# Decoder trunk on one core: both query chunks accumulated in the input loop, ten zero products ahead, latent projection after it

## The chip, the cores and the metric

The kernel runs on one core of one Trainium2 chip. The metric is the device time of one launch in microseconds (us), the median over the runs. Each core has TensorE (PE, with its weight loads shown apart as PEld), VectorE (DVE), ScalarE (ACT), GpSimd (POOL) and SyncE (SP), and 16 DMA engines that all queues share.

## The reference, cut to what matters

The reference is one inference step of a two-layer decoder trunk for 512 prompt positions and 32 sample positions (8 sequences of 4). The first layer begins with one input projection of all 544 tokens; its first columns are the query latent (256) and the key/value latent with its rotary key (128 + 32):

```python
cq, ckv, kr, hf, hi, hq, hg = jnp.split(x @ w_in, [i1, i2, i3, i4, i5, i6], axis=-1)
q = (rms_norm(cq, g_q) @ w_uq).reshape(Bn, L, MLA_HEADS, NOPE_DIM + ROPE_DIM)
ckv = rms_norm(ckv, g_kv)
kr = apply_rope(kr, cos, sin)
```

The rest of the layer (latent attention, a gated linear recurrence, output projection, layer norm, a gated ConvFFN), the second layer and the outputs follow. All of it is float32; the input width is 1024, so a projection sums over 8 chunks of 128 input channels.

## The kernel before, in words

Every float32 operand of a projection is split in two parts that TensorE takes as float32r: a rounded part `hi` (ACT copies it, L144) and the rest `lo` (DVE subtracts, L138). One step of a projection is then three products, hi*hi, hi*lo and lo*hi, which `mm3` issues (L244 to L247). Tokens are held with channels on partitions, in two halves of 256 and 288 columns (`HALF`); the last 32 columns are the sample tokens.

The change lies in the first stage of layer one (L718 to L878). SP loads the tokens as they stand in memory (`xin`: four row blocks of 128 tokens, `xins`: the 32 sample tokens) with `load_x(c0, c1)` (L736), five DMAs for one range of columns, and weights with `load_w` (L741), one DMA each into a raw tile. There are four raw tiles (`WRAW`, tag `wraw`), so a fifth weight load waits until an earlier raw tile has been split; there are seven split pairs (`WHL`). `x_in(c)` (L772) takes input chunk c: per half, TensorE transposes two blocks of 128 tokens against the identity (and the sample tokens in the second half) into PSUM, and ACT and DVE split the result into `xh`, `xl`. That is five transposes and two splits for each chunk.

The loop at L786 goes over the 8 chunks. In chunk c it calls `x_in(c + 1)`, splits the weight tiles that begin with chunk c, and then issues 18 products: 6 for the first 128 query columns (`pcq`, 256 or 288 columns wide, the weight stationary) and 12 for the latent of the four prompt token blocks (`pck[t]`, 160 columns wide, the tokens stationary). Behind the loop stand the vectors' transposes (`pv`), the latent of the sample block (`pckv4`, 24 products, L812), the evacuation of the latents on ACT (`kv_done`), the evacuation of the first query chunk (`cq_done(0)`), and the second 128 query columns as a projection of its own (L830, 48 products with two weight loads of its own). Then `filler()` issues pieces of the next projection (`phi`), which fills TensorE while the norms are worked out: `pss` (20 products with a moving operand of one column, L841) sums the squared queries, POOL takes the inverse roots for queries and latents together, DVE scales the latents (L847) and TensorE transposes them (`plat`, L864).

What sets the order: the program is written in the order above, and the framework decides each engine's order when it builds the program, by the program's order and by what it takes to be ready by then. On the chip each engine then works its own list in that order. A split of a later weight can therefore stand on ACT ahead of a split of an earlier token chunk, and waits there for its load. POOL issues the loads of the small vectors (L755 to L762) and of the page table (L833, eight DMAs that broadcast one column of the table each) on a DMA queue of its own, without waiting for the stage.

Of the kernel before, what the change touches and what calls it, by code (L numbers as in the profile page):

```python
# [10 lines left out]
F32 = mybir.dt.float32  # L11
F32R = mybir.dt.float32r
# [12 lines left out]
KC = D // 128  # L25
# [16 lines left out]
HALF = ((0, 256), (256, 288))  # L42
# [3 lines left out]
GPACE = (1,)  # L46
NORMS = (((0, (3,)), (1, (3,))), ((2, (2, 3)), (3, (2, 3)), (4, (2, 3))))
WRAW = 4
WHL = 7

C_COS = 0
# [60 lines left out]
def trunk_kernel(ctx: ExitStack, tc: tile.TileContext, a, o):  # L112
    nc = tc.nc
    PS = bass.MemoryType.PSUM
    PE, ACT, DVE, POOL = nc.tensor, nc.scalar, nc.vector, nc.gpsimd
# [31 lines left out]
    def mmtile(name):  # L147
        pools = psum["mm"]
        pool = pools[turn_[0] // 2 % len(pools)]
        turn_[0] += 1  # L150
        return pool.tile([128, 512], F32, tag="mm", name=name)

    def axtile(name):
        return psum["ax"].tile([128, 512], F32, tag="ax", name=name)
# [55 lines left out]
    def wsplit(raw, w):  # L210
        hi = wp.tile([128, 512], F32R, tag="whi", name="whi", bufs=WHL)
        lo = wp.tile([128, 512], F32R, tag="wlo", name="wlo", bufs=WHL)
        split(raw[:, :w], hi[:, :w], lo[:, :w])
        return hi, lo
# [15 lines left out]
    def wkeys(wn, c0, kch, ncol=128):  # L230
        per = 512 // ncol
        return [(wn, c0, k, min(per, kch - k), ncol) for k in range(0, kch, per)]
# [9 lines left out]
    xh, xl = [], []  # L242

    def mm3(out, lh, ll, rh, rl, first, last):  # L244
        PE.matmul(out, lh, rh, start=first, stop=False)  # L245
        PE.matmul(out, lh, rl, start=False, stop=False)  # L246
        PE.matmul(out, ll, rh, start=False, stop=last)  # L247
# [24 lines left out]
    def proj(wn, c0, hs, ls, name, halves_apart=False):  # L272
        res = {}
        for _ in proj_steps(wn, c0, hs, ls, name, res, halves_apart):
            pass
        return res["ps"]
# [4 lines left out]
    def xtok(t_, t):  # L281
        hv, s0 = ((0, 0), (0, 128), (1, 0), (1, 128), (1, 160))[t]
        return t_[hv][:, s0:s0 + 128]
# [434 lines left out]
    with tc.tile_pool(name="p1", bufs=1) as p1:  # L718
# [7 lines left out]
        with tc.tile_pool(name="pa", bufs=1) as pa:  # L726
            xin = pa.tile([128, 4, D], F32, name="xin")
            xins = pa.tile([NS, D], F32, name="xins")
            v1 = pa.tile([128, 128], F32, name="v1")
            v2 = pa.tile([128, 128], F32, name="v2")  # L730
            v3 = pa.tile([128, 128], F32, name="v3")
# [4 lines left out]
            def load_x(c0, c1):  # L736
                for i in range(4):
                    nc.sync.dma_start(xin[:, i, c0:c1], a["x_prompt"][0, i * 128:(i + 1) * 128, c0:c1])
                nc.sync.dma_start(xins[:, c0:c1], xsv[:, c0:c1])

            def load_w(key):  # L741
                w0[key] = wload(*key)

            kq = wkeys(w_in, 0, KC)
            kkv = wkeys(w_in, QR, KC, 160)
            load_x(0, 256)
            load_w(kq[0])
            load_w(kkv[0])
            load_x(256, 512)
            load_x(512, 1024)  # L750
            load_w(kkv[1])
            load_w(kq[1])
            off = 0
            for nm, ap, n in vrows:
                nc.gpsimd.dma_start(v1[off:off + n, :], ap)  # L755
# [5 lines left out]
            nc.gpsimd.dma_start(v2, fcr[nfc:nfc + 128])  # L761
            nc.gpsimd.dma_start(v3[0:n3, :], fcr[nfc + 128:264])  # L762
            V["fc"] = off
            load_w(kkv[2])

            ckv = pa.tile([128, 5, 160], F32, name="ckv")
            ss = pa.tile([128, 10], F32, name="ss")
            junk = pa.tile([128, 128], F32, name="junk")
            pcq = [mmtile(f"cq0_{h}") for h in range(2)]
            pck = [axtile(f"pckv{t}") for t in range(4)]  # L770
            wq_, wkv = [], []
            def x_in(c):  # L772
                xh.append([])
# [10 lines left out]
                    xl[c].append(l_)  # L784
            x_in(0)
            for c in range(KC):  # L786
                if c + 1 < KC:
                    x_in(c + 1)
                for keys, ws in ((kq, wq_), (kkv, wkv)):
                    for key in keys:  # L790
                        if key[2] == c:
                            hi, lo = wsplit(w0[key], key[3] * key[4])
                            ws += [(hi[:, i * key[4]:(i + 1) * key[4]], lo[:, i * key[4]:(i + 1) * key[4]])
                                   for i in range(key[3])]
                for hv, (s0, n) in enumerate(HALF):
                    mm3(pcq[hv][:, :n], wq_[c][0], wq_[c][1], xh[c][hv], xl[c][hv], c == 0, c == KC - 1)
                for t in range(4):
                    mm3(pck[t][:, :160], xtok(xh[c], t), xtok(xl[c], t), wkv[c][0], wkv[c][1], c == 0, c == KC - 1)

            nc.sync.dma_start(gkv, a["g_kvnorm"][0].partition_broadcast(128))  # L800
            nc.sync.dma_start(cst, a["cst"])
# [6 lines left out]
            def kv_done(t, p):  # L808
                ACT.copy(ckv[:, t, :], p[:, :160])
                ACT.activation(junk, ckv[:, t, 0:128], AF.Square, scale=KVR ** -0.5, accum_out=ss[:, 5 + t:6 + t])  # L810

            p = axtile("pckv4")  # L812
            for k in range(KC):
                mm3(p[:, :160], xtok(xh[k], 4), xtok(xl[k], 4), wkv[k][0], wkv[k][1], k == 0, k == KC - 1)
            kv_done(4, p)
            for t in range(4):
                kv_done(t, pck[t])
            sqs = []

            def cq_done(c, ps):  # L820
# [5 lines left out]
                split(qg, qh[c], ql[c])  # L826
                sqs.append(sq)

            cq_done(0, [pcq[hv][:, :n] for hv, (s0, n) in enumerate(HALF)])
            cq_done(1, proj(w_in, 128, xh, xl, "cq"))  # L830
            pss = axtile("pss")
            for i in range(NPAGE):
                nc.gpsimd.dma_start(ptab[16 * i:16 * (i + 1), :], a["page_table"][:, i].partition_broadcast(16))  # L833
# [763 lines left out]
```

## Time and profile before

| | us |
|---|---|
| median of 3 runs | 1415.46 |
| lowest and highest run | 1415.35, 1423.20 |
| the profiled execution's own time | 1406.60 |
| its span, first to last instruction | 1404.90 |
| around the span | 1.70 |

The profiled execution was 8.86 us shorter than the median of the timed runs. In a timeline row the first number is the start in us from the span's start, the second is how long the instruction or the merged instructions took; after them come the engine, the line, the operation, out<-in, the shape and the count; the brackets give the idle time before it and what ended that. In a windows row each engine has its busy time in the stretch and its count of instructions; the last three columns are TensorE's granted clock (1.00 is full), the mean busy share of the 16 DMA engines, and what they moved. Products on TensorE overlap, so the pace is read from the starts of successive products and not from what one took. The granted clock is put together from recorded changes of it; ahead of the first recorded change the column shows 1.00.

### The profile page before, as it was taken

What the parts mean: (1) busy time and instruction counts of PE and PEld (TensorE: products, weight loads), DVE (VectorE), ACT (ScalarE), POOL (GpSimd) and SP (SyncE); (2) the same over time, 40 slices, a digit from 0 to 9 for tenths busy, and PEclk for the clock granted to TensorE, in tenths of its full rate; (3) what the DMA queues carried; (4) which work ended last, traced back from release to release, by engine and by line L of the source; (5) the groups of instructions that cost most, each with busy time, mean ns of one, the idle gap of its engine ahead of it and who ended that gap; (6) DMA issues with size and microseconds to landing.
All of it is one profiled execution on the core that took longest, in us unless ns stands there. A gap on an engine that the chain in (4) does not pass through costs nothing.

```text
span 1404.9 us, 28697 instructions
## 1 busy us (share of the span) xinstructions
PE 1358.8 (97%) x11130; PEld 1303.9 (93%) x11130; DVE 852.3 (61%) x1672; ACT 584.0 (42%) x1439; POOL 422.8 (30%) x623
## 2 busy tenths in 40 slices
PE   6999999987999999999999999999999999999995
PEld 5999996846999999999999989999999999999995
DVE  2348766566678667667332684457786676673335
ACT  2346663445455444443322453235444444432222
POOL 4003345364725222224411110067252122240004
PEclk9999999999999999999999999999999999999997
DMA  5213123312513332232233323224133332333321
GB/s 167 58 50 84 46 66 119 116 34 76 152 30 89 90 93 85 84 97 76 80 117 90 93 79 86 86 82 128 29 102 88 92 86 73 113 106 89 88 62 64
DMA packets 218245, 120.99 MB, mean 86 GB/s; under 512 B 11488, under 2 KB 213340, under 8 KB 218108
## 3 DMA queue, kind: packets, MB, share of 16 engines
q1 hardware_dynamic: 209068, 109.89, 27.3%
q0 software_dynamic: 2144, 5.43, 1.2%
q10 hardware_dynamic: 6896, 3.82, 0.9%
q8 instruction: 88, 1.44, 0.4%
q14 instruction: 49, 0.40, 0.1%
HBM read 113.25 MB, written 5.85 MB: 85 GB/s over the span
## 4 chain that ended last, share of the span: by engine, by line
PE 90%; DVE 3%; POOL 2%; ACT 2%; DMA 2%; issue 1%; SPq 0%; ACTq 0%; DVEq 0%; POOLq 0%
PE up L245 11%; PE up L246 11%; PE up L247 11%; PE f L245 6%; PE f L246 6%; PE f L247 6%; PE m L245 2%; PE m L247 2%; PE m L246 2%; PE up L438 1%; PE up L439 1%; PE up L436 1%; POOL xs L138 1%; PE sc L1151 1%; DMA wraw<-in_w_in_ab_dram 1%
## 5 line engine op out<-in xcount | busy, mean ns | idle before, releaser
L138 DVE TENSOR_TENSOR wlo<-wraw,whi 128x512 fp32r<-128x512 f32 (+1 forms) x371 | 268.0, 726 | 369.6 <-ACT whi L144 365.8
L144 ACT CAST whi<-wraw 128x512 fp32r<-128x512 f32 (+1 forms) x371 | 224.6, 609 | 474.4 <-issue 148.2
L245 PE MATMUL f<-gh,whi 128*128 128x256 f32 (+1 forms) x704 | 204.2, 290 | 0.0
L246 PE MATMUL f<-gl,whi 128*128 128x256 f32 (+1 forms) x704 | 203.1, 289 | 0.0
L247 PE MATMUL f<-gh,wlo 128*128 128x256 f32 (+1 forms) x704 | 201.9, 287 | 0.0
L245 PE MATMUL up<-m0h,whi 128*128 128x256 f32 (+1 forms) x640 | 185.0, 289 | 0.0
L246 PE MATMUL up<-m0l,whi 128*128 128x256 f32 (+1 forms) x640 | 184.6, 289 | 0.0
L247 PE MATMUL up<-m0h,wlo 128*128 128x256 f32 (+1 forms) x640 | 184.5, 289 | 0.0
L247 PE MATMUL up<-m1h,wlo 128*128 128x256 f32 (+1 forms) x640 | 184.5, 289 | 0.0
L245 PE MATMUL up<-m1h,whi 128*128 128x256 f32 (+1 forms) x640 | 184.4, 288 | 0.0
L246 PE MATMUL up<-m1l,whi 128*128 128x256 f32 (+1 forms) x640 | 184.4, 288 | 0.0
L247 PEld LDWEIGHTS f<-gh,wlo 128*128 128x128 f32 x704 | 132.6, 188 | 0.1
L246 PEld LDWEIGHTS f<-gl,whi 128*128 128x128 f32 x704 | 132.3, 188 | 0.1
L245 PEld LDWEIGHTS f<-gh,whi 128*128 128x128 f32 x704 | 132.1, 188 | 0.1
L245 PEld LDWEIGHTS up<-m0h,whi 128*128 128x128 f32 x640 | 120.5, 188 | 0.4 <-ACT hp L621 0.3
L245 PEld LDWEIGHTS up<-m1h,whi 128*128 128x128 f32 x640 | 120.5, 188 | 0.3 <-ACT hp L621 0.2
L246 PEld LDWEIGHTS up<-m0l,whi 128*128 128x128 f32 x640 | 120.7, 189 | 0.0
L246 PEld LDWEIGHTS up<-m1l,whi 128*128 128x128 f32 x640 | 120.4, 188 | 0.0
L247 PEld LDWEIGHTS up<-m1h,wlo 128*128 128x128 f32 x640 | 120.4, 188 | 0.0
L247 PEld LDWEIGHTS up<-m0h,wlo 128*128 128x128 f32 x640 | 120.3, 188 | 0.0
L629 POOL COPY stp<-hp 128x2 f32<-128x2 f32 x88 | 40.4, 460 | 208.1 <-ACT hp L622 208.1
L620 POOL COPY hp<-pf 128x18 f32<-128x18 f32 x88 | 49.0, 563 | 130.4 <-DVE co L559 119.6
(676 smaller groups left out, 3374.4 us busy)
## 6 DMA issues: line engine op xcount, KB each, us to landing
wraw<-in_ffn_w_up_dram SPq DMA_DIRECT2D x176, 256.0 KB, 2.9
wraw<-in_ffn_w_down_dram SPq DMA_DIRECT2D x80, 256.0 KB, 2.7
wraw<-in_w_in_cd_dram SPq DMA_DIRECT2D x40, 256.0 KB, 2.8
wraw<-in_w_in_ab_dram SPq DMA_DIRECT2D x36, 256.0 KB, 2.9
wraw<-in_w_out_ab_dram SPq DMA_DIRECT2D x16, 256.0 KB, 3.0
wraw<-in_w_out_cd_dram SPq DMA_DIRECT2D x16, 256.0 KB, 3.0
sti<-in_state_hgrn_dram SPq DMA_DIRECT2D x4, 512.0 KB, 4.0
out_hg_s_dram<-sti ACTq DMA_DIRECT2D x4, 512.0 KB, 3.3
```

The source lines that it names most:

```text
L138: eng.tensor_tensor(out, in0, in1, op)
L144: ACT.copy(hi, src)
L245: PE.matmul(out, lh, rh, start=first, stop=False)
L246: PE.matmul(out, lh, rl, start=False, stop=False)
L247: PE.matmul(out, ll, rh, start=False, stop=last)
L436: PE.matmul(out, hi[:, s], xh_, start=(k == 0 and not (shared and i % 2)), stop=False, skip_group_check=shared)
L438: PE.matmul(out, hi[:, s], xl_, start=False, stop=False, skip_group_check=shared)
L439: PE.matmul(out, lo[:, s], xh_, start=False, stop=(k == KC - 1), skip_group_check=shared)
L620: POOL.tensor_copy(pre, pf[:, c, :].rearrange("p (b r) -> p b r", r=2))
L629: POOL.tensor_copy(stp[:, :, c], hp[:, HPW - 2:HPW])
L1151: PE.matmul(sc[q_][32 * bb:32 * bb + 32, :], qlt[:, 4 * g + bb, :], ltT_, start=False, stop=True)
```

## The change

The loads of the tokens are cut at columns 128, 384 and 640 (four times five DMAs where there were three times five), and a weight tile holds two input chunks of all 256 query columns (four tiles) where it held four chunks of 128 columns. The loads are issued tokens and query weights in turn, the latent weights after them. A tile of zeros is set by DVE, and ten products of 512 columns of it, into a PSUM tile that nothing reads, stand ahead of the loop. In the loop each chunk has 12 products of 256 or 288 columns, for both query chunks. The latents of all five token blocks, 24 products each, come after the loop and after the evacuation of the queries.

```diff
@@ -46,6 +46,7 @@
 GPACE = (1,)
 NORMS = (((0, (3,)), (1, (3,))), ((2, (2, 3)), (3, (2, 3)), (4, (2, 3))))
 WRAW = 4
+NWARM = 10
 WHL = 7
 
 C_COS = 0
@@ -726,6 +727,8 @@
         with tc.tile_pool(name="pa", bufs=1) as pa:
             xin = pa.tile([128, 4, D], F32, name="xin")
             xins = pa.tile([NS, D], F32, name="xins")
+            warm = pa.tile([128, 512], F32R, name="warm")
+            DVE.memset(warm.bitcast(F32), 0.0)
             v1 = pa.tile([128, 128], F32, name="v1")
             v2 = pa.tile([128, 128], F32, name="v2")
             v3 = pa.tile([128, 128], F32, name="v3")
@@ -741,15 +744,18 @@
             def load_w(key):
                 w0[key] = wload(*key)
 
-            kq = wkeys(w_in, 0, KC)
+            kq = wkeys(w_in, 0, KC, 256)
             kkv = wkeys(w_in, QR, KC, 160)
-            load_x(0, 256)
+            load_x(0, 128)
             load_w(kq[0])
-            load_w(kkv[0])
-            load_x(256, 512)
-            load_x(512, 1024)
-            load_w(kkv[1])
+            load_x(128, 384)
             load_w(kq[1])
+            load_x(384, 640)
+            load_w(kq[2])
+            load_x(640, 1024)
+            load_w(kq[3])
+            for key in kkv:
+                load_w(key)
             off = 0
             for nm, ap, n in vrows:
                 nc.gpsimd.dma_start(v1[off:off + n, :], ap)
@@ -761,13 +767,14 @@
             nc.gpsimd.dma_start(v2, fcr[nfc:nfc + 128])
             nc.gpsimd.dma_start(v3[0:n3, :], fcr[nfc + 128:264])
             V["fc"] = off
-            load_w(kkv[2])
 
             ckv = pa.tile([128, 5, 160], F32, name="ckv")
             ss = pa.tile([128, 10], F32, name="ss")
             junk = pa.tile([128, 128], F32, name="junk")
-            pcq = [mmtile(f"cq0_{h}") for h in range(2)]
-            pck = [axtile(f"pckv{t}") for t in range(4)]
+            idle = axtile("idle")
+            for i in range(NWARM):
+                PE.matmul(idle, warm[:, 0:128], warm, start=True, stop=True)
+            pcq = [[mmtile(f"cq0_{h}") for h in range(2)], [axtile(f"cq1_{h}") for h in range(2)]]
             wq_, wkv = [], []
             def x_in(c):
                 xh.append([])
@@ -784,18 +791,16 @@
                     xl[c].append(l_)
             x_in(0)
             for c in range(KC):
+                if c % 2 == 0:
+                    hi, lo = wsplit(w0[kq[c // 2]], 512)
+                    wq_ += [(hi[:, i * 256:(i + 1) * 256], lo[:, i * 256:(i + 1) * 256]) for i in range(2)]
                 if c + 1 < KC:
                     x_in(c + 1)
-                for keys, ws in ((kq, wq_), (kkv, wkv)):
-                    for key in keys:
-                        if key[2] == c:
-                            hi, lo = wsplit(w0[key], key[3] * key[4])
-                            ws += [(hi[:, i * key[4]:(i + 1) * key[4]], lo[:, i * key[4]:(i + 1) * key[4]])
-                                   for i in range(key[3])]
-                for hv, (s0, n) in enumerate(HALF):
-                    mm3(pcq[hv][:, :n], wq_[c][0], wq_[c][1], xh[c][hv], xl[c][hv], c == 0, c == KC - 1)
-                for t in range(4):
-                    mm3(pck[t][:, :160], xtok(xh[c], t), xtok(xl[c], t), wkv[c][0], wkv[c][1], c == 0, c == KC - 1)
+                for j in range(2):
+                    js = slice(j * 128, (j + 1) * 128)
+                    for hv, (s0, n) in enumerate(HALF):
+                        mm3(pcq[j][hv][:, :n], wq_[c][0][:, js], wq_[c][1][:, js], xh[c][hv], xl[c][hv],
+                            c == 0, c == KC - 1)
 
             nc.sync.dma_start(gkv, a["g_kvnorm"][0].partition_broadcast(128))
             nc.sync.dma_start(cst, a["cst"])
@@ -809,12 +814,6 @@
                 ACT.copy(ckv[:, t, :], p[:, :160])
                 ACT.activation(junk, ckv[:, t, 0:128], AF.Square, scale=KVR ** -0.5, accum_out=ss[:, 5 + t:6 + t])
 
-            p = axtile("pckv4")
-            for k in range(KC):
-                mm3(p[:, :160], xtok(xh[k], 4), xtok(xl[k], 4), wkv[k][0], wkv[k][1], k == 0, k == KC - 1)
-            kv_done(4, p)
-            for t in range(4):
-                kv_done(t, pck[t])
             sqs = []
 
             def cq_done(c, ps):
@@ -826,8 +825,16 @@
                 split(qg, qh[c], ql[c])
                 sqs.append(sq)
 
-            cq_done(0, [pcq[hv][:, :n] for hv, (s0, n) in enumerate(HALF)])
-            cq_done(1, proj(w_in, 128, xh, xl, "cq"))
+            for key in kkv:
+                hi, lo = wsplit(w0[key], key[3] * 160)
+                wkv += [(hi[:, i * 160:(i + 1) * 160], lo[:, i * 160:(i + 1) * 160]) for i in range(key[3])]
+            for j in range(2):
+                cq_done(j, [pcq[j][hv][:, :n] for hv, (s0, n) in enumerate(HALF)])
+            for t in range(5):
+                p = axtile(f"pckv{t}")
+                for k in range(KC):
+                    mm3(p[:, :160], xtok(xh[k], t), xtok(xl[k], t), wkv[k][0], wkv[k][1], k == 0, k == KC - 1)
+                kv_done(t, p)
             pss = axtile("pss")
             for i in range(NPAGE):
                 nc.gpsimd.dma_start(ptab[16 * i:16 * (i + 1), :], a["page_table"][:, i].partition_broadcast(16))
```

## Rows read from the trace of the kernel before

**Rows 1.** The page: TensorE's busy line, and the chain that ended last by engine.

```profile
PE 1358.8 (97%) x11130; PEld 1303.9 (93%) x11130; DVE 852.3 (61%) x1672; ACT 584.0 (42%) x1439; POOL 422.8 (30%) x623
...
PE 90%; DVE 3%; POOL 2%; ACT 2%; DMA 2%; issue 1%; SPq 0%; ACTq 0%; DVEq 0%; POOLq 0%
```

**Rows 2.** Windows by stage: start:end, length, busy time of each engine, clock, DMA.

```profile
core 0: us, PE busy (x) PEld busy (x) DVE busy (x) ACT busy (x) POOL busy (x), PEclk, DMA share, GB/s
0.00:8.50 8.50, 3.29 (x11) 1.81 (x11) 0.98 (x2) 2.83 (x5) 7.79 (x23) 1.00 0.70 197
8.50:18.30 9.80, 9.62 (x41) 8.89 (x41) 1.74 (x5) 0.81 (x3) 5.35 (x11) 1.00 0.53 169
18.30:24.50 6.20, 0.17 (x1) 0.00 (x0) 2.21 (x5) 2.24 (x5) 0.00 (x0) 1.00 0.40 125
24.50:52.80 28.30, 28.29 (x125) 26.23 (x125) 6.62 (x14) 6.52 (x16) 1.05 (x1) 1.00 0.25 77
52.80:62.80 10.00, 10.00 (x86) 10.00 (x86) 5.87 (x15) 6.72 (x23) 0.00 (x0) 1.00 0.42 108
...
66.40:69.90 3.50, 3.50 (x18) 3.50 (x19) 0.83 (x4) 0.37 (x1) 2.22 (x2) 0.51 0.02 6
```

**Rows 3.** Timeline of TensorE behind the loop: where each group of products begins.

```profile
54.03 0.32 PE L245 MATMUL pckv<-whi,xh 128*128 128x160 f32 x1
...
56.75 0.32 PE L245 MATMUL cq<-xh,whi 128*128 128x256 f32 x1
...
62.78 0.28 PE L245 MATMUL phi<-whi,xh 128*128 128x256 f32 x1
...
64.22 2.29 PE L841 MATMUL pss<-one,cqs 128*128 128x1 f32 x20
...
70.83 0.64 PE L864 MATMUL plat<-ident,lat 128*128 128x128 f32 x4
71.31 0.60 PE L868 MATMUL pkr<-ident,krs 128*32 128x128 f32 x4
```

**Rows 4.** Timeline of ACT around TensorE's idle stretch.

```profile
19.34 1.25 ACT L144 CAST whi<-wraw 128x480 fp32r<-128x480 f32 x2 [10.04 <-DMA wraw<-in_w_in_ab_dram]
23.14 0.46 ACT L144 CAST whi<-wraw 128x320 fp32r<-128x320 f32 x1 [2.55 <-DMA wraw<-in_w_in_ab_dram]
23.51 0.67 ACT L144 CAST xh<-px 128x256 fp32r<-128x256 f32 x2
```

**Rows 5.** Windows by what the DMA engines moved.

```profile
0.00:12.00 12.00, 6.61 (x24) 4.85 (x24) 2.72 (x6) 3.64 (x7) 10.89 (x29) 1.00 0.74 219
12.00:22.00 10.00, 6.47 (x29) 5.86 (x28) 1.35 (x2) 1.21 (x2) 2.25 (x5) 1.00 0.32 94
22.00:28.00 6.00, 3.48 (x15) 3.02 (x16) 2.62 (x6) 2.85 (x7) 0.63 (x1) 1.00 0.83 282
```

**Rows 6.** DMA view, 0 to 30 us: issues, KB each, median us to landing.

```profile
q0 software_dynamic: 608, 0.19, 3.4%
...
ptab<-in_page_table_dram POOLq DMA_DIRECT2D x8, 0.5 KB, 9.1
```

**Rows 7.** Timeline of TensorE from 24.5 us: one pass of the loop at its ends.

```profile
25.80 0.58 PE L245 MATMUL cq<-xh,whi 128*128 128x256 f32 x1
...
27.33 0.34 PE L245 MATMUL pckv<-whi,xh 128*128 128x160 f32 x1
...
29.81 1.05 PE L779 MATMUL px<-ident,xin 128*128 128x128 f32 x4
...
31.04 0.58 PE L245 MATMUL cq<-xh,whi 128*128 128x256 f32 x1
```

**Rows 8.** Timeline of SP and of POOL, the first 70 us.

```profile
0.82 1.81 SPq L738 DMA_DIRECT2D xin<-in_x_prompt_dram  x4
...
12.22 0.52 POOL L836 MEMSET kth<- 32x512 f32 x1
...
67.20 2.00 POOL L138 TENSOR_TENSOR rq<-rq,nhalf 128x10 f32<-128x10 f32 x1
```

## The prediction

> **What bounds the kernel now.** I read the page first: TensorE is busy for 97% of the span and makes up 90% of the chain that ended last [rows 1], so the time is a sum over TensorE's list, and a stage is worth what it takes from that list. The windows by stage then show that the stage touched is the worst part of it [rows 2]. To 8.5 us TensorE is busy for 3.29 us and waits for loads. From 8.5 to 18.3 it works on the first two chunks. From 18.3 to 24.5 it stands still, 0.17 us busy in 6.2. From 24.5 to 52.8 it is busy without a gap, yet gets through only 125 instructions in 28.3 us (0.226 us each); from 52.8 to 62.8 it does 86 in 10.0 us (0.116 each). The second pace is twice the first. Of the stretch 66.4 to 69.9 the view says a granted clock of 0.51, with 18 products in 3.5 us (0.194 each): that is the lower level, 1.2 GHz, and the stretch from 24.5 to 52.8 has the same slow pace although its column prints 1.00, where no change was recorded. I take all of the loop before 52.8 as run at 1.2 GHz and what comes after as 2.4 GHz. The engine went down at 66.4 behind the 20 one-column products from 64.22 [rows 3], and up at 52.8 after the loop's last chunk, the only one without transposes.
>
> The idle stretch has its reason on ACT [rows 4]: the split of the token chunk (23.51) stands behind two splits of later weights, and these waited for loads to 19.34 and 23.14. The loads were slow then: 219 GB/s over the first 12 us, 94 over the next ten, 282 after 22 us [rows 5]. In those ten us the page table's eight small loads, 0.5 KB each, are on their way (9.1 us to landing) [rows 6]. They are not part of the change.
>
> **The change part by part.** My mark is the start of the first `phi` product, 62.78 us [rows 3]: by then both query chunks and all latents are done. I work out where it lies after the change.
>
> *Pace of the parts.* At the low clock one pass has transposes from 29.81 to 31.04 (1.23 us), six query products from 25.80 to 27.33 (1.53) and twelve latent products from 27.33 to 29.81 (2.48) [rows 7]. At the high clock 24 latent products take from 54.03 to 56.75 (2.72), 48 query products from 56.75 to 62.78 (6.03), four transposes from 70.83 to 71.31 (0.48) [rows 3]. The new pass has five transposes and twelve query products: low 1.23 + 2 x 1.53 = 4.3 us, high 0.6 + 1.51 = 2.1 us. The latent, 120 products: low 120/12 x 2.48 = 24.8 us, high 5 x 2.72 = 13.6 us. The number of products on data is the same as before (96 query, 120 latent, 40 transposes); what is won is pace and idle time.
>
> *Zero products and memset.* Ten products of 512 columns, each worth two of 256: at the low clock 20 x 0.21 to 0.25 (six query products in 1.53 us, half of them 288 wide [rows 7]), 4 to 5 us; at the high one 20 x 0.126 (48 in 6.03 us), 2.5 us. They begin after the memset on DVE, which does nothing else till 7.5 us; POOL's memset of 32x512 took 0.52 us [rows 8], and I take 0.3 to 0.6 us. So they run from about 1.5 to 6 us, beside the first loads, where TensorE had 5.2 us idle [rows 2]. Then come ten transposes (up to 2.5 us, part of them before as well), and the first query product at 8.0, against 8.48 before: the first token slice is half as large, so the first weights land earlier, and this is eaten by the zero products. If that cover were gone it would cost 1 us; bounds 7.3 to 9.
>
> *Loads.* Five more token DMAs: four issues took 1.81 us on SP [rows 8], so 2.3 us more on SP, beside the transfers. Query weights are as many bytes as before (four tiles, 1.05 MB), tokens 2.23 MB, and 0.19 MB of small loads [rows 6]; the last query tile is there when 3.47 MB have moved. By the rates [rows 5] 2.63 MB are in at 12 us; at 94 GB/s the rest takes to 20.9 us, at the 219 of the start to 15.8. The latent weights (0.655 MB) wait on SP for raw tiles, then land by 22 + (4.13 - 3.57)/0.282 = 24 us. The constants now stand among them and are needed only later.
>
> *The loop.* All passes at the high clock: 8.0 + 8 x 2.1 = 24.8, and the last two passes cannot end before 15.8 or 20.9 + 1.3 (split) + 4.2 = 21.3 to 26.4; take 25. All at the low clock: 8.0 + 34.4 = 42.4, and no load is late. I take three passes low and five high: 8.0 + 12.9 + 10.5, and 1 us of waiting, 32.4. Why between: the zero products are 4 us of work without a gap right before the start, but from 6 to 8 us there are only transposes, and the loads leave gaps later; on the other side, the new passes are denser in wide products than the old ones, which went up only at 52.8.
>
> *A rule on this.* The rows show low pace after the 6.2 us of standing still, but also before it, so they don't tell whether a wait for loads costs the clock. The Trainium skill, page "TensorE: Matmul & The Clock Gate", section "HAM oscillation — how this bites in real kernels", says that a loop which waits for its loads falls back to the low clock at the waits, again and again. By that rule the zero products give nothing once the first load is late, and every pass is low; by the rows alone three of eight are. That is the second rival below.
>
> *The latent behind the loop.* 13.6 us at the high clock (24.8 at the low), and 0.3 us for three transposes of vectors. On ACT the evacuations of both query chunks come first, beside the products. What is late next: the latent of the last block is now the last product, and its chain (copy, square, POOL's 2.00 us power [rows 8], scaling) stands between it and `plat`, some 4 us. Before, `plat` came at 70.83, 8.05 us after the mark [rows 3], with the same fillers and sums between; the fillers cover 4 us, so I put 0, bounds -1 to +2.
>
> *Sum.* 32.4 + 13.9 = 46.3, against 62.78: 16.5 us less by the profiled execution, whose own time was 1406.6 with a span of 1404.9, so 1390.1. The stages behind have TensorE as their bound and move forward as they are. The timed runs, though, have a median of 1415.46, 8.86 above it. The clock's rise in this stage is the one place where I see room for that: 86 instructions ran in 10 us after it [rows 2], and had it come later they would have taken up to 10 us more. The new order leaves less to that, and I give it half, 4.4 us. So 1415.46 - 16.5 - 4.4 = 1394.6 us.
>
> **The rivals.**
> 1. *The clock comes up with the zero products and holds.* Loop end 25, latent 13.9: the mark at 38.9, 23.9 less, with the 4.4 us 1387.2. For it: 4 us of work without a gap, and 24 latent products in a row ran at 2.4 GHz at 54 us. Against it: few products between 6 and 8 us, and loads at 94 GB/s from 12 us.
> 2. *Waits for loads, and the clock with them.* As before, ACT's list puts splits of later weights ahead of a token chunk's [rows 4]; all seven pairs fit, so it can stand till the last latent weight at 24 us. With three passes done, the rest begins at 24.9: three low, two high, 42.0; the latent 13.9: 55.9, 6.9 less, with 2 us of the other term 1406.6. All eight passes low gives nearly the same, 42.4 + 13.9 = 56.3. For it: 6.2 us lost in just this way. Against it: loads come in the order of use now.
> 3. *Slower: the latent runs at the low clock.* Its 160-column products stood between 24.5 and 52.8 at 0.21 us each and never ran fast there; gathered in one block, they would stay so if TensorE enters them low: 42.4 + 24.8 + 0.6 = 67.8, 5.0 late, and the first `phi` products at the low clock another 1.4: 1421.9. It decides at the first latent product: low there, this case; high there, one of the others. Against it: the same products kept the high clock from 52.8 to 56.75.
>
> That the zero products raise nothing at all is no case of its own: the forecast has three passes low already.
>
> **How the numbers follow.** Forecast 0.50 (its own range 1388 to 1401), first rival 0.22, second 0.21, third 0.07. A measurement of this kernel tells a change of about 1%, 14 us, from none. Faster by more than that (under 1401.3): nearly all of the forecast, 0.46, the first rival, and 0.04 of the second: 0.72. Within 1%: 0.04 + 0.17 + 0.01 = 0.22. Slower: 0.06. The range runs from 1380 (first rival with all of the 8.86 us and some) to 1411 (second rival with nothing of it, and bounds of the small terms), and leaves out the third rival and the edges.
>
> **What would show it.** Right: ten products on `warm` from about 1.5 us; no stretch over 4 us without TensorE work after 8 us; passes 4.3 us apart at first and 2.1 later; 24 latent products in 2.7 us; first `phi` product between 43 and 50 us; the rest of the trace moved by as much. Wrong: `phi` before 41 (first rival) or after 52 (second); 24 latent products in 5 us (third); a first query product after 9.5; `plat` more than 10 us behind the first `phi`; or a later stage that gives the time back.

## The result and the profile after

| | us |
|---|---|
| kernel before, median of 19 runs beside the changed one | 1417.34 |
| changed kernel, median of 19 runs | 1407.18 (1405.58 to 1415.15) |
| changed / before | 0.9928, 95% interval 0.9913 to 0.9944 |
| changed kernel, profiled execution | 1406.99, span 1405.3 |

The change wins 10.2 us, 0.7%, where 20.9 us against the median of 1415.46 was forecast. The interval shows a real gain, but it is half of the forecast and under the 1% (14 us) that the prediction had named as the least it could tell from none.

The page of the changed kernel, the same two lines as in [rows 1]:

```profile
PE 1354.3 (96%) x11140; PEld 1299.0 (92%) x11140; DVE 850.7 (61%) x1673; ACT 583.7 (42%) x1439; POOL 419.4 (30%) x623
...
PE 89%; DVE 3%; POOL 2%; ACT 1%; DMA 1%; issue 1%; another core or an unknown queue 1%; SPq 0%; DVEq 0%; ACTq 0%; POOLq 0%
```

New in the chain is 1% of "another core or an unknown queue", some 14 us. First the stage that was changed, TensorE's timeline (the kernel before in [rows 3]):

```profile
1.53 3.98 PE L776 MATMUL idle<-warm 128*128 128x512 f32 x10 [1.53 <-DVE warm L731]
...
9.27 0.82 PE L246 MATMUL cq<-xh,whi 128*128 128x256 f32 x2
...
22.37 0.30 PE L786 MATMUL px<-ident,xin 128*128 128x128 f32 x1 [1.74 <-DMA xin<-in_x_prompt_dram]
23.45 0.33 PE L786 MATMUL px<-ident,xin 128*128 128x128 f32 x1 [0.79 <-DMA xin<-in_x_prompt_dram]
...
33.34 0.32 PE L246 MATMUL pckv<-whi,xh 128*128 128x160 f32 x1
...
46.79 0.32 PE L246 MATMUL phi<-whi,xh 128*128 128x256 f32 x1
```

The mark, the first `phi`, is at 46.79; 46.3 was forecast. The windows by stage (the kernel before in [rows 2]) show the clock, third column from the end:

```profile
8.00:14.80 6.80, 6.80 (x27) 5.79 (x28) 2.37 (x6) 1.96 (x5) 5.87 (x12) 0.50 0.60 174
14.80:20.40 5.60, 5.60 (x44) 5.17 (x42) 2.27 (x5) 1.97 (x5) 0.00 (x0) 1.00 0.31 95
20.40:23.50 3.10, 0.57 (x5) 0.19 (x2) 0.00 (x0) 0.00 (x0) 0.00 (x0) 1.00 0.87 278
25.10:28.50 3.40, 3.40 (x16) 2.99 (x15) 3.40 (x8) 2.44 (x7) 0.00 (x0) 0.50 0.85 268
28.50:46.80 18.30, 18.30 (x161) 18.09 (x159) 7.07 (x14) 9.64 (x27) 0.61 (x1) 1.00 0.35 96
```

The loop is at 1.2 GHz to 14.8 and at 2.4 to 20.4, then stands idle for 2.5 of the 3.1 us to 23.5, waiting for the last token columns. Behind that wait it is at 1.2 GHz from 25.1 to 28.5, and then it holds 2.4. So the stage gains what was forecast: 62.78 - 46.79 = 16.0 us between the two profiled executions. The next group shows where that goes. The first two lines are the kernel before, the last two the changed one: the same products of the linear recurrence.

```profile
212.06 0.46 PE L1264 MATMUL pd<-hq,hth 128*32 128x32 f32 x32 [0.70 <-DVE hth L1252]
214.01 0.45 PE L1287 MATMUL plv<-hq,hth 128*32 128x16 f32 x32
```

```profile
195.47 0.46 PE L1271 MATMUL pd<-hq,hth 128*32 128x32 f32 x32 [0.68 <-DVE T L1258]
...
204.83 0.63 PE L1294 MATMUL plv<-hq,hth 128*32 128x16 f32 x32 [7.33 <-DVE hq L139]
```

At `pd` the changed kernel is 16.6 us ahead, at `plv` 9.2. The view of waits for 195 to 206 us of the changed kernel (us in total, times, longest) names the place. "Remote" stands where the profile shows no releaser; only one core runs this program:

```profile
ACT th L1246 <- remote: 9.5, 1, 9.5
DVE SB L1272 <- remote: 7.6, 1, 7.6
...
PE plv L1294 <- DVE hq L139: 7.3, 1, 7.3
```

and the windows say what works meanwhile (PE, PEld, DVE, ACT, POOL):

```profile
197.50:203.80 6.30, 0.00 (x0) 0.00 (x0) 0.00 (x0) 0.00 (x0) 5.38 (x10) 0.63 0.85 285
203.80:209.40 5.60, 4.57 (x78) 4.25 (x79) 3.32 (x12) 1.31 (x3) 4.86 (x10) 0.50 0.06 22
264.90:266.80 1.90, 0.23 (x3) 0.00 (x0) 0.00 (x0) 0.00 (x0) 0.91 (x1) 1.00 0.84 308
267.40:274.20 6.80, 6.44 (x55) 5.97 (x56) 2.55 (x10) 0.76 (x3) 0.00 (x0) 0.50 0.30 110
```

For 6.3 us TensorE, VectorE and ScalarE do nothing at all; only GpSimd works, issuing the gathers of the cache pages. VectorE's `SB` waits for products that were done at 195.9, and it starts 1.7 us after the issue of the last gather has ended:

```profile
201.19 0.95 POOL L1083 DMA_INDIRECT kr<-in_cache_krope_dram,pidx  x1 [0.30 <-issue]
203.85 0.30 DVE L1272 COPY_PREDICATED SB<-msk,pd 128x128 f32<-128x128 uint8 x1 [7.61 <-remote]
```

Behind it TensorE runs at 1.2 GHz. The same comes, shorter, at 265, at the second group of gathers. In the profiled execution of the kernel before the gathers passed with no such stretch. I call it a standstill. Of the 16.6 us ahead 6.5 are left behind the first standstill and its slow stretch, 0.1 behind the second (at 322 us of the kernel before), and none at the end: 1406.99 against 1406.60. Yet the medians differ by 10.2. So either the new code makes the standstills, or the one execution profiled before was not like its timed runs.

### The profile page after: what moved, and what is told of

Read it like the earlier page. It is cut to its first block, busy times and chain, and to the rows that moved or that the text cites. A ratio compares the mean times of both kernels' runs of the same rounds, so it can differ in the third digit from the quotient of the medians.

```text
span 1405.3 us, 28725 instructions
## 1 busy us (share of the span) xinstructions
PE 1354.3 (96%) x11140; PEld 1299.0 (92%) x11140; DVE 850.7 (61%) x1673; ACT 583.7 (42%) x1439; POOL 419.4 (30%) x623
## 4 chain that ended last, share of the span: by engine, by line
PE 89%; DVE 3%; POOL 2%; ACT 1%; DMA 1%; issue 1%; another core or an unknown queue 1%; SPq 0%; DVEq 0%; ACTq 0%; POOLq 0%
PE up L246 11%; PE up L247 11%; PE up L248 11%; PE f L246 6%; PE f L247 6%; PE f L248 6%; POOL xs L139 2%; PE m L246 1%; PE m L248 1%; PE m L247 1%; PE up L439 1%; DMA xin<-in_x_prompt_dram 1%; PE up L440 1%; PE up L437 1%; PE sc L1158 1%
## 5 line engine op out<-in xcount | busy, mean ns | idle before, releaser
L139 DVE TENSOR_TENSOR wlo<-wraw,whi 128x512 fp32r<-128x512 f32 (+2 forms) x371 | 267.5, 725 | 365.7 <-ACT whi L145 359.7
L145 ACT CAST whi<-wraw 128x512 fp32r<-128x512 f32 (+2 forms) x371 | 224.9, 609 | 474.7 <-issue 152.0
```

The costliest lines, as they stand in the source:

```text
L139: eng.tensor_tensor(out, in0, in1, op)
L145: ACT.copy(hi, src)
```

## The experiments

With the one above there are six series of runs, the five later ones on five chips; each has its own runs of the kernel before. "Own" is the time of the profiled execution, "median" the median less that of the kernel before in the same series, so that a gain is negative. "Plain loads" and the other variants are told below the table.

| kernel | first phi | own | own - phi | median |
|---|---|---|---|---|
| before, first profile | 62.78 | 1406.60 | 1343.8 | |
| changed, first profile (standstills) | 46.79 | 1406.99 | 1360.2 | -10.2 |
| before again | 55.81 | 1399.36 | 1343.6 | |
| before, third | 63.46 | 1408.22 | 1344.8 | |
| changed again | 46.86 | 1389.91 | 1343.1 | -8.7 |
| before, plain loads | 60.37 | 1405.50 | 1345.1 | +1.1 |
| changed, plain loads, series without standstills | 46.28 | 1392.41 | 1346.1 | -8.5 |
| changed, plain loads, series with | 45.89 | 1397.70 | 1351.8 | -14.9 |
| changed, no zero products (standstills) | 49.18 | 1415.35 | 1366.2 | -4.3 |
| before + zero products (standstills) | 53.08 | 1414.41 | 1361.3 | -0.9 |
| changed, old load cuts (standstills) | 49.59 | 1416.42 | 1366.8 | -6.2 |
| changed order alone | 49.99 | 1393.00 | 1343.0 | -5.4 |
| before, page loads late | 43.01 | 1387.51 | 1344.5 | -9.8 |
| changed, page loads late (standstills) | 40.85 | 1403.16 | 1362.3 | -13.5 |
| changed, page loads late, another series (standstills) | 41.33 | 1407.05 | 1365.7 | -15.0 |
| changed, page loads late, no zero products | 45.26 | 1388.64 | 1343.4 | -12.3 |
| changed, page loads late, gathers held back | 42.59 | 1392.08 | 1349.5 | -10.6 |

**Both kernels unchanged, again.**

> The kernel before, unchanged, for a second profile and the clock of each run. Theory A (the standstill of TensorE, VectorE and ScalarE that the profile of the changed kernel shows at 197.5 to 203.9 us, while GpSimd issues the gathers, befalls either kernel from one execution to the next): this second profile of the kernel before shows a standstill of over 3 us during the gathers at 209 to 220 us in which neither of the three engines works, its time is 1413 to 1420 us, and its clock is below the 0.993 of the first profile. Theory B (the standstill belongs to the changed kernel alone, because its instructions meet the gathers at another point): none here, the span as in the first profile within 3 us.

> The changed kernel, unchanged, for a second profile. Theory A: the standstills move or change their length from one profile to the next (the first had 6.4 us at 197.5 and 1.7 us at 265.1), and the first phi stays at 46.8 us within 1 us. Theory B: 6.4 us again at 197.5 within 1 us. Time 1407 us, within 3.

Neither theory: no standstill in either kernel, and both some 17 us faster than in the first series (the changed one 1390.8 against 1407.2). The changed kernel in the stretch of its former standstill:

```profile
197.50:203.80 6.30, 6.30 (x142) 5.54 (x141) 5.47 (x19) 2.75 (x10) 5.08 (x8) 1.00 0.79 248
```

So the new code alone does not bring them: the changed kernel, unchanged, has none here. Nor are they its alone: the kernel before with ten zero products (below) has one of the same length. The kernel before itself was never profiled in a series that has them; that its runs there hold them too is read from its medians, 1416.67 to 1417.34 us in those series and 1399.4 to 1400.7 in the others. But the kernel before has another first `phi`, 55.81 in place of 62.78. Its windows:

```profile
18.70:23.30 4.60, 0.00 (x0) 0.00 (x0) 0.00 (x0) 0.00 (x0) 0.00 (x0) 0.82 0.45 133
23.30:35.30 12.00, 9.08 (x40) 8.22 (x40) 5.79 (x12) 5.33 (x12) 1.03 (x1) 0.50 0.58 173
35.30:55.80 20.50, 20.50 (x170) 19.87 (x170) 8.81 (x22) 9.66 (x31) 0.00 (x0) 1.00 0.27 74
```

The idle stretch is there, but the clock is up at 35.3, not at 52.8. The pair's medians differ by 8.7 us, as their marks do (55.81 - 46.86 = 9.0).

> The kernel before, unchanged, for a third profile. The theory by now has two parts. First: the point at which TensorE's clock comes up for good in the early stage differs from one execution of this kernel to the next (35.3 and 52.8 us in two profiles), and the first phi with it (55.8 and 62.8); it should lie between 53 and 65 us again, and the time without standstills is that mark plus 1343.5 us, within 1 us. Second: standstills at the gathers add 16 to 23 us to any of these kernels in some series of runs and nothing in others; if the runs of this series have them, this profile shows 5 to 7 us in which TensorE, VectorE and ScalarE do nothing, while GpSimd issues gathers, and a time of the mark plus 1360 to 1367 us. The rival is that the standstills come with the new code alone: none here, whatever the other kernels of the series show.

First `phi` 63.46, time 1408.22 (the mark plus 1344.8, 0.3 us beyond the 1 us allowed), no standstill. Its windows:

```profile
17.80:21.50 3.70, 0.00 (x0) 0.00 (x0) 0.00 (x0) 0.06 (x1) 0.00 (x0) 0.83 0.39 111
21.50:54.40 32.90, 30.09 (x133) 28.04 (x134) 9.44 (x19) 9.71 (x24) 1.04 (x1) 0.50 0.28 83
54.40:63.40 9.00, 9.00 (x77) 9.00 (x77) 5.17 (x14) 5.63 (x19) 0.00 (x0) 1.00 0.44 117
```

Here the clock is at 1.2 GHz for 33 us and up at 54.4, much as in the first profile (by the pace of its products up at 52.8). In nine of the ten rows without standstills the time is the mark plus 1343.0 to 1346.1 (the tenth is the one with the gathers held back). So I read the timed runs, which have no trace, as marks: the kernel before at its median of 1399.5 stands near 56, the changed one (1390.8) near 47. Of 79 runs of the kernel before in the three series without standstills 18 are at 1404 us or more: the profile that the prediction stood on was one of the late quarter. The changed kernel's runs spread over 3.2 us, those of the kernel before over 12.8 in the same series.

**Plain loads in place of the first gathers.** Left out is the look-up of the page table for four of the eight sequences.

```diff
-  nc.gpsimd.indirect_dma_start(lt, None, clat, off)
-  nc.gpsimd.indirect_dma_start(kr[:, bb, :], None, ckro, off)
+  if g == 0:
+      nc.sync.dma_start(lt, clat[128 * b:128 * b + 128, :])
+      nc.sync.dma_start(kr[:, bb, :], ckro[128 * b:128 * b + 128, :])
+  else:
+      nc.gpsimd.indirect_dma_start(lt, None, clat, off)
+      nc.gpsimd.indirect_dma_start(kr[:, bb, :], None, ckro, off)
```

> The changed kernel, with the eight gathers of the first group of sequences replaced by eight plain loads of as many bytes from SyncE (this leaves out the look-up of the page table for these four sequences). If what GpSimd writes while it issues indirect gathers holds the engines up, the standstill at 197.5 is gone, the second at 265 (still a gather) may stay, and the time is 6 to 13 us lower than the changed kernel's: 1395 to 1401 us. If the bytes themselves (the DMA traffic of 2.6 MB) hold the engines up, the standstill stays and the time is within 3 us of 1407.

> The kernel before with the same replacement. Theory A: its timed runs had the standstill too, so they fall by 6 to 13 us, to 1404 to 1411 us, and the gap to the changed kernel with plain loads is that of the early stage. Theory B: within 3 us of the kernel before, and the changed kernel with plain loads lies 14 to 18 us below this one.

There was nothing to take away in this series: a gain of 8.5 us with the changed kernel, a loss of 1.1 with the kernel before. In two more series, free of standstills as well, the changed kernel with plain loads gained 8.3 and 9.0 (marks 47.60 and 46.58). The last series had them. Beside the kernel with plain loads ran, as the control, the changed kernel with late page loads (below) and all its gathers.

> The changed kernel with plain loads for the first four sequences' gathers (leaves out the look-up of the page table for these), a last time, for a series with standstills: none before 250 us and a median 18 to 24 us below the kernel before's if the gathers' issue makes them; one of 4 us or more at the first hand-over and 8 to 12 us below if not. In a series without them 8 to 10 us below, and the point is left open.

> The changed kernel with late page loads, for its place beside the kernel before in a second series: the first phi at 40 to 43 us and, as each time so far that mark plus 1343.5 us without standstills, a median 12 to 16 us below the kernel before's. If the series has standstills, this profile has them too, at about 192 and 261 us, and stands beside the one with plain loads as the control.

The control, its two standstills:

```profile
192.40:198.60 6.20, 0.00 (x0) 0.00 (x0) 0.01 (x1) 0.00 (x0) 5.28 (x9) 0.86 0.85 276
267.30:268.90 1.60, 0.01 (x1) 0.00 (x0) 0.00 (x1) 0.00 (x0) 0.67 (x1) 1.00 0.92 305
```

and with plain loads:

```profile
192.40:198.60 6.20, 5.25 (x98) 4.82 (x97) 5.66 (x20) 2.51 (x9) 6.20 (x10) 1.00 0.96 318
197.40:203.80 6.40, 6.40 (x141) 5.69 (x141) 5.29 (x21) 2.16 (x7) 2.24 (x6) 1.00 0.83 286
257.70:259.30 1.60, 0.00 (x1) 0.00 (x0) 0.05 (x1) 0.01 (x1) 0.68 (x1) 1.00 0.90 317
```

Without GpSimd's gathers the first standstill is gone, at more traffic (318 GB/s against 276); the second, where gathers are still issued, stays. So the gathers on GpSimd's queue make it, and not the bytes moved. Whether it is their issue or the queue's own work behind it is not shown: the control's first standstill, too, ends 1.6 us after the last issue has. This is one profile of each. The median gained 14.9 us, not the 18 to 24 expected: the second group still costs. Why this comes in three series and not in the other three, no run tells; each of the five later series had a chip of its own, so the chip can't be told from other causes.

> The changed kernel with late page loads, and the first gathers held back: each sequence's two gathers wait for a small memset that VectorE does in its turn, so that they go out in two portions (after the first hand-over from TensorE to VectorE, and a step later) instead of one of 10 us. In a series with standstills: if the issue of the gathers itself holds the signals up, the standstill breaks into pieces of 1 to 4 us at the new places, each ending with an issue; if it belongs to the place in the program, it stays 6 us at the first hand-over. In a series without them: no standstill over 1 us, the first phi at 40 to 42 us and a median 12 to 16 us below the kernel before's.

```diff
+ if g == 0:
+     tc.keep_in_program_order(DVE.memset(lt[:, 0:1], 0.0))
  nc.gpsimd.indirect_dma_start(lt, None, ...)
  nc.gpsimd.indirect_dma_start(kr[:, bb, :], None, ...)
+ if g == 0:
+     yield
```

In a series without standstills: none, as expected, but the gain was 10.6 us, less than the 12 to 16, and the time behind the mark 6 us more than in the other rows. TensorE waits 1.9 us before 199.2, and from 199.6 to 206.5 its clock is 0.51. Whether holding the gathers back breaks a standstill up stays untried.

**The parts of the change.** One taken out, or done alone.

```diff
-NWARM = 10
+NWARM = 0
```

> The changed kernel without its ten zero products. Theory C (they raise TensorE's clock early and at the same point of every execution, and that is most of the gain): without them the granted clock reaches 1.0 only behind 25 us, the first phi moves from 46.8 to 50 to 57 us, the timed runs spread over 6 us or more as those of the kernel before do (12.8 us), and the median is 0 to 5 us below the kernel before's. Theory O (the order is the gain: no latent matmuls between loads, both query chunks on one landed chunk): the zero products took 4 us of idle time and nothing else, the first phi stays within 2 us of 46.8, and the median stays 7 to 11 us below the kernel before's.

```diff
+ warm = pa.tile([128, 512], F32R, name="warm")
+ DVE.memset(warm.bitcast(F32), 0.0)
...
+ idle = axtile("idle")
+ for i in range(10):
+     PE.matmul(idle, warm[:, 0:128], warm, start=True, stop=True)
  pcq = [mmtile(f"cq0_{h}") for h in range(2)]
```

> The kernel before with the ten zero products alone. Theory C: the first phi, at 62.8, 55.8 and 60.4 us in three profiles of the kernel before (and with plain loads), comes at 48 to 52 us, the spread falls under 5 us and the median is 5 to 9 us lower. Theory O: the clock falls again while TensorE waits for loads at 18 to 24 us, the first phi lies at 54 to 60 us and the median within 2 us of the kernel before's.

```diff
- load_x(0, 128); load_w(kq[0]); load_x(128, 384); load_w(kq[1])
- load_x(384, 640); load_w(kq[2]); load_x(640, 1024); load_w(kq[3])
+ load_x(0, 256); load_w(kq[0]); load_w(kq[1])
+ load_x(256, 512); load_x(512, 1024); load_w(kq[2]); load_w(kq[3])
```

> The changed kernel with the input loads cut as before (256, 256 and 512 columns, the two first weight tiles behind the first cut). The cuts as a part of the gain: the first query product starts 1.5 to 3 us later (10.7 to 12 us, as twice the bytes must land before it), the first phi 1 to 3 us later, the median 1 to 3 us above the changed kernel's place (8.7 us below the kernel before). The cuts as nothing: the slow stretch of the loads between 12 and 22 us decides when the last columns land in either order, the first phi within 1 us of 46.8 and the median within 1 us of that place.

> The changed order of TensorE's work alone: both query chunks together and the latents behind them, but without the zero products and with the input loads cut as before. Without the zero products the first phi came at 49.2 us, with the old cuts at 49.6, against 46.8 with both. If these two are independent: 50 to 53 us and a median 2 to 5 us below the kernel before's, spread over 6 us. If one covers for the other (a product that waits for its load needs no clock): 49 to 50 us.

The last is the old cuts and no zero products together. The marks are 49.18, 53.08, 49.59 and 49.99, the gains 4.3, 0.9, 6.2 and 5.4 us. All four kernels share one picture, shown here for the kernel before with zero products:

```profile
5.10:14.50 9.40, 7.92 (x56) 6.50 (x54) 3.12 (x7) 2.73 (x7) 7.74 (x15) 1.00 0.78 239
...
14.50:22.00 7.50, 0.00 (x0) 0.00 (x0) 0.00 (x0) 0.04 (x1) 1.03 (x2) 0.79 0.28 80
...
18.80:32.50 13.70, 8.70 (x37) 7.62 (x38) 5.35 (x11) 5.17 (x11) 1.06 (x1) 0.50 0.68 204
32.50:53.10 20.60, 20.60 (x172) 19.97 (x172) 9.03 (x22) 9.66 (x31) 0.00 (x0) 1.00 0.27 74
```

The clock comes up and is lost over a wait for loads: TensorE stands idle for 9.2 us here (14.5 to 23.7), 5.5 with the old cuts, 5.3 with the order alone and 2.3, in pieces, without zero products. So the zero products do raise it, from 5.1 us, where it rose at 11.9 with the order alone and at 16.6 without zero products; but in the old order they hand that back at the wait. There theory O was right (median within 0.9 us; the mark of 53.08 is just under its 54). In the new order neither theory was: the mark of 49.18 lies between them, 2.4 us behind 46.79, and the clock rose at 16.6 and not behind 25, yet the gain fell to 4.3 us as theory C had it. The order alone carries 5 to 6 of the 9 us, cuts and zero products some 3 us together. Its mark of 49.99 is the one that the second reading expected, but not by one covering for the other: from there the cuts alone give 0.8 us (49.18), the zero products alone 0.4 (49.59), both 3.2, so that each needs the other. These are single profiles in different series. With the old cuts the first product came at 8.82, not late as expected; the price is the wait for the last columns. And the order makes the stage repeat: alone it spreads over 2.8 us (1392.2 to 1395.0), not the 6 expected, where the kernel before spreads over 15 in the same series.

**The page-table loads.** In both orders the traffic falls to 94 to 115 GB/s between 12 and 22 us. The eight loads were put behind the latent stage:

```diff
- for i in range(NPAGE):
-     nc.gpsimd.dma_start(ptab[16 * i:16 * (i + 1), :], ...)
...
  vals4(0)
  filler(2)
+ for i in range(NPAGE):
+     tc.keep_in_program_order(
+         nc.gpsimd.dma_start(ptab[16 * i:16 * (i + 1), :], ...))
```

> The changed kernel with its eight page-table loads issued behind the latent stage (about 60 us) instead of at 7.5 to 12.7 us. If these loads, of 0.5 KB each in 4-byte pieces, are what slows the traffic from 220 to 100 GB/s between 12 and 22 us, the last input columns land at 16 to 18 us instead of 23.5, the idle time of 1.8 us before 23.5 goes, and the first phi comes 1.5 to 4 us earlier (43 to 45 us), the median 10 to 12.5 us below the kernel before's. If the slow stretch has another cause (the many small packets of the vectors' loads, the number of open transfers), the rate between 12 and 22 us stays under 130 GB/s and nothing moves by over 0.7 us.

> The kernel before with its page-table loads issued behind the latent stage, nothing else. Loads as the bound of the old loop: the last input columns land 5 to 7 us earlier, the standstill between 18 and 24 us shrinks to under 2 us, the first phi comes at 46 to 54 us, and the median is 4 to 9 us below the kernel before's, as much as the whole change gave. The clock as the bound: the loop runs at 1.2 GHz as long as before, the first phi stays at 53 us or later, and the median falls by under 3 us.

12 to 22 us and the stage up to the first `phi`, first the changed kernel with late page loads, then the kernel before with them:

```profile
12.00:22.00 10.00, 10.00 (x74) 9.16 (x75) 7.12 (x16) 5.58 (x14) 0.00 (x0) 1.00 0.91 283
4.40:40.80 36.40, 34.12 (x264) 31.23 (x263) 16.70 (x34) 17.99 (x48) 5.84 (x12) 1.00 0.62 184
```

```profile
12.00:22.00 10.00, 10.00 (x65) 9.14 (x65) 5.29 (x11) 4.73 (x11) 0.95 (x1) 1.00 0.97 301
16.60:43.00 26.40, 26.40 (x218) 25.31 (x218) 13.02 (x31) 12.85 (x38) 0.95 (x1) 1.00 0.41 118
```

94 GB/s [rows 5] becomes 301, 115 becomes 283. In these ten us TensorE has no wait, and the clock stays up once it has risen. The loads were the bound of both loops; both marks are earlier than either reading had them. This one move gives the old kernel 9.8 us (ratio 0.993, 0.9906 to 0.9954), as much as the whole change. Both together win 13.5 us (0.9898, 0.9868 to 0.9929) in one series and 15.0 (0.9881, 0.9816 to 0.9946) in another: the best version that was run.

> The changed kernel with the page-table loads behind the latent stage and without the ten zero products. With late page loads and zero products the clock rose at 4.4 us and held to 45 us, and the first phi came at 40.9. If the zero products only mattered because the loads then left gaps, the loop without gaps raises the clock by itself: clock up before 14 us, first phi at 40 to 43 us, median within 2 us of 13.5 us below the kernel before. If they are what raises it: as in the changed kernel without them, the rise comes at 16 us or later, first phi at 44 to 48 us, median 4 to 7 us above that place.

Without zero products the clock rises at 17.9, where with them it is up for good from 4.4 and 12.6, and from 15.3 in the kernel with the gathers held back, whose early stage is the same; the mark is 45.26 in place of 40.85, 41.33 and 42.59. The gain of 12.3 us is yet close to that with them (13.5 and 15.0, in other series). The mark speaks for the second reading (they raise it), the median for 1 to 3 us at most.

## Why the prediction was wrong, point by point

- *The stage itself.* Right, in the main. First product 9.27 (8.0, bounds 7.3 to 9: just outside), passes 4.1 us low and 2.3 high (4.3 and 2.1), zero products 3.98 us (4 to 5), waiting 2.5 us (1), loop end 33.3 (32.4), 120 latent products 13.45 us at 2.4 GHz (13.6), mark 46.79 (46.3), `plat` 7.05 us behind it (8.05, bounds -1 and +2). The loads were later than forecast: the last token columns landed at 23.5, where the query weights, issued behind them, were to be there by 15.8 to 20.9.
- *The range and the rivals.* 1407.2 us lies outside the forecast's own range (1388 to 1401) and inside the wide one (1380 to 1411). The rivals' marks were 38.9, 55.9 and 67.8. The second's time, 1406.6, is within 0.6 us of the 1407.2 measured, by luck: its mark is 9 us too late, and the 62.78 that it was taken from was late as well.
- *The clock.* Three passes low and five high was near: low to 14.8 and again from 25.1 to 28.5, behind a wait. The prediction tied the rise at 52.8 to the last chunk, which has no transposes; in the second profile of the kernel before it rose at 35.3, inside the loop. The Trainium skill, "TensorE: Matmul & The Clock Gate", section "HAM oscillation — how this bites in real kernels", says that a loop which waits for its loads starts cold again behind each wait. The rows agree that the clock fell in or behind each long wait of the loop where its changes are on record (waits of 2.5 to 9.2 us); that every pass is then low, as the prediction drew from it, they don't show: here it came back after 3.4 us, in the second and third profile of the kernel before after 14 and 34.
- *"against 62.78: 16.5 us less by the profiled execution".* This is the term that failed. 62.78 was taken for the kernel before as such; it was one late execution. At the median its mark is near 56, and 56 - 47 = 9 us is about what was measured, 8.7 to 10.2. This put the gain 6.8 us too high, and the next term another 4.4: 11.2 of the 20.9 us forecast.
- *"The clock's rise in this stage is the one place where I see room for" the 8.86 us; "I give it half, 4.4 us".* Wrong in sign. The profiled execution was already at the late end, so the median had to be some 7 us earlier by this stage, not later. The 8.86 us are put down to the standstills: 16.7 us more behind the mark (1360.2 - 1343.5, from the changed kernel's profile), less the 6.8 us by which that execution was late, make 9.9. They lie in a stage that the change doesn't touch, and cost both kernels about the same, by the medians of the series. Taken away, the forecast's own working gives 1415.5 - (56.0 - 46.3) = 1405.8 us; 1407.2 was measured.
- *"The stages behind ... move forward as they are."* Right, though the first pair of traces shows what the prediction had named as a sign of being wrong, a later stage that gives the time back: to 195 us the shift is 16.0 to 17.0 us, then the standstills take it. In the second pair it is 9.6 to 9.8 us from there to 970 us and 9.1 behind it.
- *"They are not part of the change", of the page-table loads.* True, and why a third of what was to be had was left (8.7 to 10.2 us gained, 13.5 to 15.0 with them moved): the last columns still landed at 23.5.

## What to carry to other kernels

Before the difference to a profile's stage is promised as a gain, ask whether that stage repeats: where a clock rises inside it, one execution shows one of several outcomes (here marks of 55.8 to 63.5 us), and a gap between the profile and the timed median must be found in the trace, not given to the stage at hand. The stage here paid twice for a wait for loads, for the wait and for the clock behind it (2.5 us and 3.4 at 1.2 GHz in the changed kernel), so the slow stretch of the DMA view is worth asking about first; moving eight loads of 0.5 KB did as much here as reordering all the work.

## What the runs showed that was not expected

**Eight small loads from GpSimd slowed the loads beside them without using the DMA engines much.** The DMA view of the changed kernel, 12.3 to 22.8 us, when the page-table loads are on their way (packets, MB, share of the engines' time):

```profile
q1 hardware_dynamic: 1291, 1.42, 41.8%
q0 software_dynamic: 208, 0.00, 1.5%
```

Their own packets fill 1.5% of the engines' time, while the other queue's share is 41.8%, and 91.7% with the loads moved. SyncE's issue slows too, first with them, then with the loads moved:

```profile
13.04 2.08 SPq L742 DMA_DIRECT2D xins<-in_x_sample_dram  x1
15.17 5.62 SPq L208 DMA_DIRECT2D wraw<-in_w_in_ab_dram  x4
```

```profile
12.13 0.43 SPq L742 DMA_DIRECT2D xins<-in_x_sample_dram  x1
12.60 3.40 SPq L208 DMA_DIRECT2D wraw<-in_w_in_ab_dram  x4
```

One issue took 2.08 us in place of 0.43. The Trainium skill, "DMA: Bandwidth & Descriptors", section "Why small descriptors are slow (HBM only)", puts the price of small descriptors in a fixed overhead per packet and in the bytes of the descriptors themselves. By the share above that price is small here, and the cost fell on the loads beside them. By what path is open, and so is whether the slow issue holds the transfers up or they the issue.

**GpSimd's gathers can stop three engines.** In three of six series there are up to 6.4 us without any instruction on TensorE, VectorE and ScalarE while the gathers are issued, and 1.2 GHz behind it; with the second group and all that follows it costs 17 to 23 us of 1400 (own - phi, 1360.2 to 1366.8 against 1343.5). The other three series show none, with the changed kernel the same in both.
